# Adding the result onto the residual in DRAM with accumulating DMAs, and four reorderings, in a one-core encoder layer

## The chip, the cores and the metric

The kernel runs on one NeuronCore of a Trainium2 chip. The metric is device time in microseconds (us) of one execution. Three runs of the kernel before took 1187.17, 1188.81 and 1190.94 us; the median is 1188.81 us.

Engines are named as in the profile: PE is the matrix engine (PEld its weight loads), DVE, ACT and POOL are the vector, scalar and GpSimd engines, SP issues DMAs. SPq, ACTq and POOLq are the DMA queues of SP, ACT and POOL.

## What is computed

One layer of a streaming encoder on 1024 prompt frames and 64 frames of a running stream, 1088 columns together, all in float32. Cut to what matters here:

```
hn = rmsnorm(x, g_pre1)
z = hn @ w_in                                  # [gate | xa | u | v], 4 x 512 columns
xa_c = causal_dwconv(xa); h = rg_lru(xa_c)     # gates r, i: sigmoid of block-diagonal products of xa_c
ya = rmsnorm(h * gelu(gate), g_out_a)
yb = rmsnorm(u * (w_s @ layernorm(v) + b_s), g_out_b)
x  = x + rmsnorm([ya, yb] @ w_o, g_post1)      # residual
hn2 = rmsnorm(x, g_pre2)
f  = (gelu(conv(hn2 @ w_up)[:, :3072]) * conv(hn2 @ w_up)[:, 3072:]) @ w_down
x  = x + rmsnorm(f, g_post2)                   # the output y; w_down is 3072 x 1024
```

## The kernel before, in words

Features lie on the 128 partitions, frames along the free dimension (1088 columns). Every float32 operand of a product is split into two parts of a reduced float32 type, `hi` (a rounding copy on ACT, L140) and `lo` (the remainder, a subtraction on DVE, L142 or L144), and a product is three matmuls: hi by hi, hi by lo, lo by hi. So every weight tile (128 x 1024, 512 KB, name `wraw`) is loaded by a DMA on SP, then split into `whi` and `wlo` before PE can use it.

A scheduler places instructions: the kernel text says what depends on what, and each engine then gets a fixed list that it works through in order. A DMA in SP's list that waits holds up all DMAs behind it in that list, the weight loads too. All large tiles come from one pool of 47 buffers.

The stages, in order of time:

- **Front** (to about 45 us of the span). For each of 8 input tiles `xr` (544 KB) ACT and DVE make `xh` and `xl`, and PE forms v in two passes over k = 0 to 7 (`v_mm`); weights `w_v` come as three tiles of 512 KB, one for two k. `gate_const` (L351) makes the constant `cst` of the v gate from one matmul `wsum` and four DVE operations.
- **Mixers.** `xa_tile` makes xa and its convolution `xc` on DVE (L487 to L489) and splits it into `ch` and `cl` there (L491 to L493); `lru_gates` multiplies those on PE and takes sigmoids `r` and `ig` on ACT; `u_tile` first multiplies its gate by the row scale `rbt`, on POOL (L536). Then the output projection; `post1` forms the residual x and stores it to a DRAM buffer `xd` (L708).
- **Up-projection** (about 400 to 900 us), a Strassen-like scheme of 7 products; its gated results and their sums go to the DRAM buffer `bd`.
- **Down-projection** (about 880 us to the end), the same scheme: 7 products in the order of `DOWN` (L40), each named by its operand of `bd` and its weight part: A11, S2 = A21 + A22 - A11, S3, A22, A12, S1 = A21 + A22, S4 = A12 - S2. Each product has 6 steps n; a step is `down_step` (48 matmuls of 272 columns), then `wmake(n + 3)` (split of the weights), `bmake(n + 6)`, `wload(n + 4)` and `bload(n + 7)`. In the product S2 `wload` loads three tiles, `wmake` forms S1 and S2 on DVE and stores both to the DRAM buffer `sd` by POOL; the products S1 and S4 read them back. `down_evac` adds the products into the 8 accumulators `facc`.
- **Finish.** `finish` does a quarter of the columns: `load_xn` reads the residual back from `xd` (SP), one matmul group sums the squares, POOL takes the power -1/2, then for 8 row tiles DVE multiplies (L1120), POOL or DVE adds to the residual (L1121), and SP stores groups of three tiles to the output (L1097). Two quarters run during the sixth product, the third in the middle of the seventh, whose columns are done in two parts of 284 and 260 (`COLS2`; its PSUM tile is `lps`, that of the others `dps`). `finish_last` does the last quarter at the very end, on DVE and POOL together.

Of the kernel before, what the change touches and what calls it, by code (L numbers as in the profile page):

```python
# [14 lines left out]
P = 128  # L15
# [24 lines left out]
DOWN = [("B11", "A11"), ("T2", "S2"), ("T3", "S3"), ("T4", "A22"), ("B21", "A12"), ("T1", "S1"), ("B22", "S4")]  # L40
# [27 lines left out]
def layer_kernel(ctx: ExitStack, tc, xT, w_fm, w_v, w_o, w_up, w_down, w_g, w_s, par, bc, yT, small, vn_out):  # L68
# [332 lines left out]
    for k in range(1, KD):  # L401
# [3 lines left out]
        if k == 3:  # L405
            gate_const()
# [67 lines left out]
    def xa_tile(t, fill=()):  # L474
# [92 lines left out]
    def seq(*fs):  # L567
# [8 lines left out]
    lru_tile(1)  # L576
    u_tile(1)
    xa_tile(3, lru_gates(2))
    lru_tile(2)
    u_tile(2)  # L580
# [96 lines left out]
    xd = drp.tile([P, KD, T], F32, tag="xd", name="xd")  # L677
# [15 lines left out]
    def post1(c, mix, tiles, ssq):  # L693
# [8 lines left out]
        for m in range(KD):  # L702
# [276 lines left out]
    def wload(n):  # L979
# [6 lines left out]
        for src in {"A11": (a11,), "S2": (a21, a22, a11), "S3": (a11, a21), "A22": (a22,), "A12": (a12,),  # L986
# [5 lines left out]
    def wmake(n):  # L992
# [4 lines left out]
        src = raw[0]  # L997
        if DOWN[p][1] == "S2":
            a21, a22, a11 = raw
            nc.vector.tensor_tensor(a22, a21, a22, op=ALU.add)  # L1000
            nc.gpsimd.dma_start(sd[0, i], a22)
            nc.vector.tensor_tensor(a11, a22, a11, op=ALU.subtract)
            nc.gpsimd.dma_start(sd[1, i], a11)
            src = a11
        elif len(raw) == 2:
            nc.vector.tensor_tensor(raw[0], raw[0], raw[1], op=ALU.subtract)  # L1006
# [11 lines left out]
    for j in range(NPRE, NF):  # L1018
        hooks = ()
        if j == NF - 1:  # L1020
# [4 lines left out]
                     [call(bmake, 3), call(bload, 5), call(wmake, 2)])  # L1025
# [6 lines left out]
    wload(3)  # L1032
    bmake(5)
    bload(6)
# [27 lines left out]
    def down_evac(p, m, ps):  # L1062
# [6 lines left out]
        if p == 0:  # L1069
            facc[m] = big_tile(name="facc")[:, :T]  # L1070
            for c, (a, b) in enumerate(CC):
                with tc.high_priority(offset=PRI):
                    nc.scalar.activation(facc_cols(m, a, b), ps[c], AF.Copy)
        elif p == 1:
            add(m, 1, m, 0)
        elif p == 2:
            facc[m + 4] = big_tile(name="facc")[:, :T]
            add(m + 4, 1, m, 1)
        elif p == 3:
            add(m + 4, 0, m + 4, 1)  # L1080
        elif p == 4:
            add(m, 0, m, 0)
# [3 lines left out]
        if p == 3 or p == 5:  # L1086
            h = 0 if p == 3 else HT
            for a, b in CC:
                sq_add(m + 4, h + a, h + b)
        if p == 4:  # L1090
            for a, b in CC:
                sq_add(m, a, b)

    def out_dma(m, cols, xn, queue):
        if m % 3 == 2 or m == KD - 1:
            g, n = m // 3, m % 3 + 1
            queue.dma_start(yT[:, 3 * g:3 * g + n, cols], xn[g][:, :n, :])  # L1097

    def load_xn(cols):
        w = cols.stop - cols.start  # L1100
        xn = [big_tile(shape=(P, 3, w), name="xn") for _ in range(3)]
        for q in range(3):
            e = min(3 * q + 3, KD)
            nc.sync.dma_start(xn[q][:, :e - 3 * q, :], xd[:, 3 * q:e, cols])
        return xn

    def finish(cols, xn=None):
        w = cols.stop - cols.start
        xn = xn or load_xn(cols)
        yield  # L1110
# [6 lines left out]
        for m in range(KD):  # L1117
            f = facc[m][:, cols]
            x = xn[m // 3][:, m % 3, :]
            nc.vector.scalar_tensor_tensor(f, f, pv("g_post2", m), rr, op0=ALU.mult, op1=ALU.mult)  # L1120
            (nc.vector if m % 3 == 2 else nc.gpsimd).tensor_tensor(x, x, f, op=ALU.add)  # L1121
            out_dma(m, cols, xn, nc.sync)
            if m % 2 == 1:
                yield

    def scale_f(m, cols):
        f = facc[m][:, cols]
        nc.scalar.activation(f, f, AF.Copy, scale=pv("g_post2", m))

    def finish_last(cols, xn, more):  # L1130
# [5 lines left out]
        for n, m in enumerate(range(KD)):  # L1136
            f = facc[m][:, cols]
            x = xn[m // 3][:, m % 3, :]
            mul, add = LAST_ENG[m]
            e = {"v": nc.vector, "g": nc.gpsimd}  # L1140
# [21 lines left out]
    last_p = len(DOWN) - 1  # L1162
    for n in range(6 * last_p):
        if n == 6 * last_p - 6:
            gens2.append(finish(slice(*COLS1[0])))
# [120 lines left out]
```

## Time and profile before

| what | value |
|---|---|
| median of three runs | 1188.81 us |
| the profiled execution's own time | 1188.03 us |
| its span | 1186.3 us |
| PE busy, mean granted clock | 1137.9 us (96%), 0.983 |
| DVE, ACT, POOL busy | 861.6, 531.3, 178.2 us |
| HBM read, written | 110.65 MB, 38.85 MB |

PE is busy in 96% of the span, so a microsecond in which PE waits, or runs at the lower of its two clock levels, is nearly always a microsecond of the kernel. The other engines matter only where PE waits for them. The 48 us in which PE is not busy are at the two ends and in a few waits, which the rows below list.

### The profile page before, as it was taken

The page shows a single profiled execution, that of the slowest core. Times are in us where ns is not written, and L with a number is a line of the kernel's source. Part 1 is how long each engine was busy: PE and PEld are TensorE (multiplying, and loading weights), DVE is VectorE, ACT ScalarE, POOL GpSimd, SP SyncE. Part 2 cuts the span into 40 slices and gives each one's busy share as a digit, 9 for nine tenths or more (in the row PEclk, how much of TensorE's full clock was granted, in tenths as well). Part 3 has the DMA queues.
Part 4 walks back from the last instruction along what each step waited for, and adds up shares of the span by engine and source line. Part 5 has one row for each costly group of instructions (what it writes and reads, how often), then busy time and mean ns, then how long its engine had stood idle before and what let it go on. Part 6 is the DMA issues. An engine that isn't in the chain of part 4 may idle for free. (4 is left out here: it accounts for less than half of the span.)

```text
span 1186.3 us, 20679 instructions
## 1 busy us (share of the span) xinstructions
PE 1137.9 (96%) x8420; PEld 1115.8 (94%) x8420; DVE 861.6 (73%) x1374; ACT 531.3 (45%) x868; POOL 178.2 (15%) x292
## 2 busy tenths in 40 slices
PE   8998999999999999999999999999999999999675
PEld 6798999999998999999999999999999999999675
DVE  7567666866687889787887778778779574656745
ACT  7212567544445545444444445444464233433321
POOL 0214001110000122221021111111221100002203
PEclk9999999999999999999999999999999999999878
DMA  8110111221333132232132223223169985543562
GB/s 309 36 41 18 37 36 36 72 92 42 99 116 116 36 120 93 93 119 93 50 134 98 80 99 123 76 78 128 61 241 402 418 332 206 196 154 111 195 226 76
DMA packets 54000, 150.85 MB, mean 127 GB/s; under 512 B 5488, under 2 KB 22384, under 8 KB 53904
## 3 DMA queue, kind: packets, MB, share of 16 engines
q1 hardware_dynamic: 44784, 119.18, 28.8%
q0 software_dynamic: 8496, 29.81, 6.4%
q8 instruction: 66, 1.08, 0.4%
q10 hardware_dynamic: 624, 0.53, 0.2%
q14 instruction: 30, 0.25, 0.1%
HBM read 110.65 MB, written 38.85 MB: 126 GB/s over the span
## 5 line engine op out<-in xcount | busy, mean ns | idle before, releaser
L898 PE MATMUL up<-bh,wop 128*128 128x274 f32 x2464 | 472.7, 290 | 0.0
L898 PEld LDWEIGHTS up<-bh,wop 128*128 128x128 f32 x2464 | 389.4, 189 | 1.8 <-ACT uraw L912 1.3
L898 PE MATMUL up<-bl,wop 128*128 128x274 f32 x1232 | 356.8, 290 | 0.0
L898 PEld LDWEIGHTS up<-bl,wop 128*128 128x128 f32 x1232 | 233.3, 189 | 0.0
L1057 PE MATMUL dps<-gh,whi 128*128 128x272 f32 x576 | 121.1, 290 | 3.6 <-ACT whi L140 3.6
L1057 PE MATMUL dps<-gh,wlo 128*128 128x272 f32 x576 | 119.6, 290 | 0.9 <-DVE wlo L142 0.8
L1057 PE MATMUL dps<-gl,whi 128*128 128x272 f32 x576 | 120.4, 289 | 0.0
L140 ACT ACTIVATE whi<-wraw 128x1024 fp32r<-128x1024 f32 x70 | 73.0, 1050 | 87.3 <-DVE wraw L1006 37.2
L142 DVE TENSOR_TENSOR wlo<-wraw,whi 128x1024 fp32r<-128x1024 f32 x70 | 85.1, 1220 | 26.0 <-ACT whi L140 25.8
L140 ACT ACTIVATE wop<-wsum 128x512 fp32r<-128x512 f32 x88 | 53.0, 627 | 107.6 <-DVE wsum L854 105.3
L1057 PEld LDWEIGHTS dps<-gh,whi 128*128 128x128 f32 x576 | 91.2, 189 | 4.1 <-ACT whi L140 4.1
L912 ACT ACTIVATE uraw<-up 128x274 f32<-128x274 f32 x176 | 65.7, 389 | 64.6 <-PE up L898 64.2
L1057 PEld LDWEIGHTS dps<-gh,wlo 128*128 128x128 f32 x576 | 90.6, 189 | 1.8 <-DVE wlo L142 1.8
L1057 PEld LDWEIGHTS dps<-gl,whi 128*128 128x128 f32 x576 | 91.3, 190 | 0.0
L798 DVE SCALAR_TENSOR_TENSOR yg<-uraw,pt,yg 128x1090 f32<-128x1090 f32 (+1 forms) x48 | 64.8, 1350 | 26.5 <-ACT yg L796 26.5
L917 DVE TENSOR_TENSOR uraw<-up,uraw 128x274 f32<-128x274 f32 x132 | 56.3, 438 | 33.5 <-PE up L898 30.6
L641 PE MATMUL ops<-yh,whi 128*128 128x274 f32 (+1 forms) x256 | 75.2, 294 | 0.0
L641 PE MATMUL ops<-yl,whi 128*128 128x274 f32 (+1 forms) x256 | 73.8, 288 | 0.0
L641 PE MATMUL ops<-yh,wlo 128*128 128x274 f32 (+1 forms) x256 | 73.7, 288 | 0.0
L185 POOL TENSOR_TENSOR rs<-v,mhalf 92x3 f32<-92x3 f32 (+4 forms) x20 | 21.8, 1089 | 326.6 <-DVE v L184 326.6
L424 PE MATMUL ps<-xh,whi 128*128 128x364 f32 (+3 forms) x296 | 69.6, 330 | 0.0
L798 DVE SCALAR_TENSOR_TENSOR yv<-uraw,pt,yv 128x1090 f32<-128x1090 f32 (+1 forms) x48 | 64.7, 1347 | 4.8 <-ACT yv L796 4.6
(225 smaller groups left out, 2225.7 us busy)
## 6 DMA issues: line engine op xcount, KB each, us to landing
wraw<-in_w_down_dram SPq DMA_DIRECT2D x54, 512.0 KB, 8.3
wraw<-in_w_up_dram SPq DMA_DIRECT2D x48, 512.0 KB, 3.8
graw<-bd SPq DMA_DIRECT2D x42, 544.0 KB, 6.7
bd<-yg POOLq DMA_DIRECT2D x36, 272.0 KB, 3.1
bd<-ta POOLq DMA_DIRECT2D x24, 272.0 KB, 3.2
bd<-tb POOLq DMA_DIRECT2D x24, 272.0 KB, 3.2
wraw<-in_w_fm_dram SPq DMA_DIRECT2D x12, 512.0 KB, 3.5
sd<-wraw POOLq DMA_DIRECT2D x12, 512.0 KB, 7.6
```

The costliest lines, as they stand in the source:

```text
L140: nc.scalar.activation(hi, src, AF.Copy, scale=1.0 if scale is None else scale)
L142: nc.vector.tensor_tensor(lo, src, hi.bitcast(F32), op=ALU.subtract)
L185: nc.gpsimd.tensor_tensor(out, v[:n[0], :n[1]], mhalf[:n[0], :n[1]], op=ALU.pow)
L424: nc.tensor.matmul(ps[c], wt[:, k * P:(k + 1) * P], at[k][:, cols], start=(k == 0 and q == 0), stop=(k == KD - 1 and q == 2))
L641: nc.tensor.matmul(ps, wt[:, i * 256 + mi * P:i * 256 + (mi + 1) * P], a[k, c], start=(first and i == 0 and j == 0), stop=(last and i == 3 ...
L798: nc.vector.scalar_tensor_tensor(y[:, d:TG], x[:, :TG - d], tap(2 - d), y[:, d:TG], op0=ALU.mult, op1=ALU.add)
L898: nc.tensor.matmul(dst[c], wt[:, k * P:(k + 1) * P], at[:, fourth(k)], start=(start and k == 0 and q == 0), stop=(k == 3 and q == 2), skip ...
L912: nc.scalar.activation(dst[c], src[c], AF.Copy)
L917: nc.vector.tensor_tensor(dst[c], src[c], p[c], op=ALU.add)
L1057: nc.tensor.matmul(ps, wt[:, k * 256 + mi * P:k * 256 + (mi + 1) * P], at[:, o + a:o + b], start=(first and k == 0 and q == 0), stop=(last ...
```

## The change

`DOWN` is put in a new order, with the product A12 second and the product of S2 third. `operand(n)` makes weights one step sooner (`wmake(n + 4)`, `wload(n + 5)`). S1 is no longer formed on DVE: six DMAs on SP copy A21 from DRAM to `sd`, and six accumulating DMAs on POOL add A22 to it there. They are written in the loop of the up-projection, but the scheduler decides their place. The residual goes to the output tensor itself instead of `xd`; `finish` and `finish_last` scale their results and add them to it by accumulating DMAs on POOL, and the loads of `xn`, the adds and the stores on SP are gone. In the front `gate_const` comes at k = 1 instead of k = 3, the split of `xc` becomes a function of its own, `xa_split`, called later, the multiplication by `rbt` goes from POOL to DVE, and the first broadcast matmul of `rstd_tail` keeps its place in program order.

```diff
-DOWN = [("B11", "A11"), ("T2", "S2"), ("T3", "S3"), ("T4", "A22"), ("B21", "A12"), ("T1", "S1"), ("B22", "S4")]
+DOWN = [("B11", "A11"), ("B21", "A12"), ("T2", "S2"), ("T3", "S3"), ("T4", "A22"), ("T1", "S1"), ("B22", "S4")]
@@ rstd_tail
+            if b == 0:
+                tc.keep_in_program_order(mm)
@@ second pass of v
         if k == 1:
             stats_x()
-        if k == 3:
             gate_const()
@@ xa_tile
+        lru[t] = [xc]
+
+    def xa_split(t):
+        xc = lru[t][0]
         ch, cl = big_tile(F32R, name="ch"), big_tile(F32R, name="cl")
         for g, d in PIECES:
-            split(ch[:, d], cl[:, d], xc[:, g])
+            tc.keep_in_program_order(nc.scalar.activation(ch[:, d], xc[:, g], AF.Copy))
+            nc.vector.tensor_tensor(cl[:, d], xc[:, g], ch[:, d].bitcast(F32), op=ALU.subtract)
@@ u_tile
-        nc.gpsimd.tensor_tensor(sh, sh, rbt, op=ALU.mult)
+        nc.vector.tensor_tensor(sh, sh, rbt, op=ALU.mult)
@@ the calls
+    xa_split(0)
     xa_tile(1, ...)
-    u_tile(0, lru_gates(0))
+    u_tile(0, lru_gates(0) + [lambda: xa_split(1)])
...
@@ post1
-                nc.sync.dma_start(xd[:, 4 * g:4 * g + 4, qs(c)], v4(xt[g], w))
+                nc.sync.dma_start(yT[:, 4 * g:4 * g + 4, qs(c)], v4(xt[g], w))
@@ wload, wmake
-        for src in {"A11": (a11,), "S2": (a21, a22, a11), ...
+        for src in {"A11": (a11,), "S2": (s1, a11), ...
+        if len(raw) == 2:
+            nc.vector.tensor_tensor(src, src, raw[1], op=ALU.subtract)
         if DOWN[p][1] == "S2":
-            a21, a22, a11 = raw
-            nc.vector.tensor_tensor(a22, a21, a22, op=ALU.add)
-            nc.gpsimd.dma_start(sd[0, i], a22)
-            nc.vector.tensor_tensor(a11, a22, a11, op=ALU.subtract)
-            nc.gpsimd.dma_start(sd[1, i], a11)
-            src = a11
+            nc.gpsimd.dma_start(sd[1, i], src)
@@ loop of the up-projection, j = NPRE to NF - 1
+        i = j - NPRE - 2
+        if 0 <= i < 6:
+            nc.sync.dma_start(sd[0, i], w_down[1, 0, i])
+        if 1 <= i < 7:
+            nc.gpsimd.dma_start(sd[0, i - 1], w_down[1, 1, i - 1], accum_op=ALU.add, max_dma_last_dim=1024)
@@ finish
-        xn = xn or load_xn(cols)
-        yield
...
             nc.vector.scalar_tensor_tensor(f, f, pv("g_post2", m), rr, op0=ALU.mult, op1=ALU.mult)
-            (nc.vector if m % 3 == 2 else nc.gpsimd).tensor_tensor(x, x, f, op=ALU.add)
-            out_dma(m, cols, xn, nc.sync)
+            nc.gpsimd.dma_start(yT[:, m, cols], f, accum_op=ALU.add)
@@ finish_last
-            e[mul].tensor_tensor(f, f, bp if mul == "v" else rr, op=ALU.mult)
-            e[add].tensor_tensor(x, x, f, op=ALU.add)
-            out_dma(m, cols, xn, nc.scalar if m // 3 == 1 else nc.sync)
+        for g, q in ((1, nc.sync), (0, nc.scalar)):
+            for m in range(4):
+                f = fg[g][:, m, :]
+                nc.vector.tensor_tensor(f, f, bp, op=ALU.mult)
+            nc.gpsimd.dma_start(yT[:, 4 * g:4 * g + 4, cols], fg[g], accum_op=ALU.add)
@@ steps of the down-projection
+    def operand(n):
+        wmake(n + 4)
+        bmake(n + 6)
+        wload(n + 5)
+        bload(n + 7)
```

Left out of the diff: `down_evac` and `sq_add` follow the new order of the products (the first product is now copied to both halves of `facc` by 8 more ACT copies of 272 columns), and `scale_f` writes the last quarter into two packed tiles `fg`.

**SP, the first DMAs of the program.** `xr` are input tiles, `wraw` weights, `sd` is the DRAM buffer of S1 and S2. Before, from the sixth DMA on:

```order
L302 DMA pt<-in_par_dram 128x432
L321 DMA xr<-in_xT_dram 128x1088 x2
L166 DMA wraw<-in_w_v_dram 128x1024 x3
L166 DMA wraw<-in_w_g_dram 128x1024
L321 DMA xr<-in_xT_dram 128x1088 x2
```

Now, from the same DMA on:

```order
L304 DMA pt<-in_par_dram 128x432
L1031 DMA sd<-in_w_down_dram 16x8192 x2
L323 DMA xr<-in_xT_dram 128x1088
L1031 DMA sd<-in_w_down_dram 16x8192 x2
L323 DMA xr<-in_xT_dram 128x1088
L1031 DMA sd<-in_w_down_dram 16x8192 x2
L166 DMA wraw<-in_w_v_dram 128x1024 x3
L166 DMA wraw<-in_w_g_dram 128x1024
L323 DMA xr<-in_xT_dram 128x1088 x2
```

The six copies of A21 (512 KB each) stand at the head of the program: two ahead of the input tile of k = 1, four ahead of that of k = 2, six ahead of the weights of k = 2. The six accumulating DMAs are now the first DMAs of POOL's list, each behind the copy that it adds to.

**SP, the loads around the last product.** `graw` is the operand from `bd`, `xn` the residual, `out_dram` the output. Before:

```order
L1104 DMA xn<-xd 128x3x272 x2
L1104 DMA xn<-xd 128x2x272
L1097 DMA out_dram<-xn 128x3x272
L989 DMA wraw<-in_w_down_dram 128x1024
L989 DMA wraw<-sd 128x1024
L972 DMA graw<-bd 128x1088
L1097 DMA out_dram<-xn 128x3x272
L1097 DMA out_dram<-xn 128x2x272
L989 DMA wraw<-in_w_down_dram 128x1024
L989 DMA wraw<-sd 128x1024
```

Now:

```order
L997 DMA wraw<-in_w_down_dram 128x1024
L997 DMA wraw<-sd 128x1024
L980 DMA graw<-bd 128x1088
L997 DMA wraw<-in_w_down_dram 128x1024
L997 DMA wraw<-sd 128x1024
L980 DMA graw<-bd 128x1088
```

In the down-projection SP's list now holds loads of operands alone; the additions to the output are DMAs of POOL.

**ACT, the gates of the first head group.** `ch` is the rounded `xc` of the tile in question, `r` and `ig` the sigmoids that free the PSUM tile `gps`. Before:

```order
L140 ACTIVATE ch<-xc 128x1024
L140 ACTIVATE ch<-xc 128x64
L140 ACTIVATE whi<-wraw 128x1024
L140 ACTIVATE ch<-xc 128x1024
L140 ACTIVATE ch<-xc 128x64
L140 ACTIVATE whi<-wraw 128x1024
L507 ACT_TABLE_LOAD
L507 ACTIVATE r<-gps,pt 128x364 x2
```

Now:

```order
L498 ACTIVATE ch<-xc 128x1024
L498 ACTIVATE ch<-xc 128x64
L140 ACTIVATE whi<-wraw 128x1024 x2
L513 ACT_TABLE_LOAD
L513 ACTIVATE r<-gps,pt 128x364 x2
```

The split of the second tile's `xc` no longer stands ahead of the first tile's sigmoids; it comes behind all six of them.

## Rows read from the trace of the kernel before

**Rows 1.** Page, the span in 40 slices of 29.7 us, in tenths.

```profile
DMA  8110111221333132232132223223169985543562
```

**Rows 2.** Waits of PE, largest: waiter, released by, total us, times, longest us.

```profile
PE lps L1057 <- ACT whi L140: 16.0, 4, 7.1
PE gps L505 <- ACT r L507: 3.7, 1, 3.7
PE dps L1057 <- ACT whi L140: 3.6, 3, 1.8
PE bp L392 <- DVE cst L355: 2.9, 1, 2.9
```

**Rows 3.** Windows of PE: stretch, us, busy (instructions), granted clock, DMA share, GB/s.

```profile
1088.60:1092.60 4.00, 3.96 (x19) 0.57 0.99 334
...
1121.40:1126.40 5.00, 4.97 (x19) 0.50 0.86 257
1130.30:1136.70 6.40, 6.19 (x23) 0.50 1.07 382
1140.80:1146.80 6.00, 5.98 (x25) 0.50 0.69 238
1150.00:1155.00 5.00, 5.00 (x42) 1.00 0.01 3
```

**Rows 4.** Waits of SP's DMA queue from 880 us on.

```profile
SPq L1097 <- DVE xn L1121: 68.9, 5, 30.4
```

**Rows 5.** Timeline of SP, 1057 to 1088 us: start, us, instruction.

```profile
1058.29 1.56 SPq L1104 DMA_DIRECT2D xn<-xd  x3
1086.13 0.96 SPq L1097 DMA_DIRECT2D out_dram<-xn  x2
1087.18 0.53 SPq L989 DMA_DIRECT2D wraw<-sd  x1
```

**Rows 6.** Timeline of DVE, 1112 to 1122 us.

```profile
1113.19 5.39 DVE L1120 SCALAR_TENSOR_TENSOR facc<-facc,pt,rrf 128x272 f32<-128x272 f32 x8
```

**Rows 7.** Windows of all: us, PE, PEld, DVE, ACT, POOL busy, PE clock, DMA, GB/s.

```profile
8.00:17.00 9.00, 8.31 (x32) 6.32 (x31) 7.70 (x22) 8.29 (x12) 0.00 (x0) 1.00 1.02 415
17.00:26.00 9.00, 8.93 (x39) 6.95 (x38) 9.00 (x9) 6.46 (x7) 0.31 (x1) 1.00 1.03 354
...
900.00:960.00 60.00, 58.11 (x455) 57.03 (x454) 41.57 (x41) 17.79 (x22) 7.70 (x15) 1.00 1.02 411
```

**Rows 8.** Timeline of ACT, front: the splits of `w_v` and of a late input tile.

```profile
13.37 3.05 ACT L140 ACTIVATE whi<-wraw 128x1024 fp32r<-128x1024 f32 x3
...
25.22 1.21 ACT L140 ACTIVATE xh<-xr,gp 128x1088 fp32r<-128x1088 f32 x1 [1.97 <-DMA xr<-in_xT_dram]
```

**Rows 9.** Timeline of PE, front: the first matmuls of k = 2 and k = 5.

```profile
16.91 0.40 PE L288 MATMUL vps<-whi,xh 128*128 128x512 f32 x1
...
29.78 0.86 PE L288 MATMUL vps<-whi,xh 128*128 128x512 f32 x3
```

**Rows 10.** Timeline, 96 to 115 us: POOL, DVE and PE around the first gates.

```profile
96.30 11.65 POOL L536 TENSOR_TENSOR s<-s,rbt 128x1088 f32<-128x1088 f32 x4 [9.87 <-DVE s L383]
...
102.05 8.44 DVE L489 SCALAR_TENSOR_TENSOR xc<-xa,pt,xc 128x1090 f32<-128x1090 f32 x3
...
114.61 0.43 PE L505 MATMUL gps<-ch,whi 128*128 128x360 f32 x1 [3.73 <-ACT r L507]
```

**Rows 11.** Window just behind that wait, columns as in rows 7.

```profile
115.50:119.90 4.40, 4.40 (x18) 4.12 (x17) 1.21 (x1) 2.10 (x4) 0.00 (x0) 0.61 0.00 0
```

**Rows 12.** Page, another operation of that form: count, busy us, mean ns.

```profile
L798 DVE SCALAR_TENSOR_TENSOR yg<-uraw,pt,yg 128x1090 f32<-128x1090 f32 (+1 forms) x48 | 64.8, 1350 | 26.5 <-ACT yg L796 26.5
```

**Rows 13.** Timeline of DVE, end: first and last operations behind the sum of squares.

```profile
1177.68 0.76 DVE L1141 TENSOR_TENSOR facc<-facc,bp 128x260 f32<-128x260 f32 x2 [2.41 <-ACT rrf L207]
...
1182.27 0.73 DVE L1142 TENSOR_TENSOR xn<-xn,facc 128x260 f32<-128x260 f32 x1
```

**Rows 14.** DMA issues, 1173 to 1187 us: KB each, median us to landing.

```profile
out_dram<-xn SPq DMA_DIRECT2D x1, 390.0 KB, 2.7
```

More of the change, by code (lines that the diff above doesn't have):

```diff
@@ L576, in layer_kernel @@
     lru_tile(1)
+    xa_split(2)
     u_tile(1)
@@ L579, in layer_kernel @@
     lru_tile(2)
+    xa_split(3)
     u_tile(2)
@@ L675, in o_mm @@
         return mix, tiles, ssq
-    xd = drp.tile([P, KD, T], F32, tag="xd", name="xd")
     hn = {}
@@ L985, in wload @@
         wraw[n] = []
-        for src in {"A11": (a11,), "S2": (a21, a22, a11), "S3": (a11, a21), "A22": (a22,), "A12": (a12,),
+        for src in {"A11": (a11,), "S2": (s1, a11), "S3": (a11, a21), "A22": (a22,), "A12": (a12,),
                     "S1": (s1,), "S4": (a12, s2)}[DOWN[p][1]]:
@@ L1031, in layer_kernel @@
     opb.clear()
-    wload(3)
+    wmake(2)
     bmake(5)
+    wload(4)
+    wmake(3)
     bload(6)
@@ L1070, in down_evac @@
             facc[m] = big_tile(name="facc")[:, :T]
-            for c, (a, b) in enumerate(CC):
-                with tc.high_priority(offset=PRI):
-                    nc.scalar.activation(facc_cols(m, a, b), ps[c], AF.Copy)
+            for h in range(2):
+                for c, (a, b) in enumerate(CC):
+                    with tc.high_priority(offset=PRI):
+                        nc.scalar.activation(facc_cols(m, h * HT + a, h * HT + b), ps[c], AF.Copy)
         elif p == 1:
-            add(m, 1, m, 0)
+            add(m, 0, m, 0)
         elif p == 2:
+            add(m, 1, m, 1)
+        elif p == 3:
             facc[m + 4] = big_tile(name="facc")[:, :T]
             add(m + 4, 1, m, 1)
-        elif p == 3:
+        elif p == 4:
             add(m + 4, 0, m + 4, 1)
-        elif p == 4:
-            add(m, 0, m, 0)
         elif p == 5:
@@ L1085, in down_evac, with finish @@
             add(m, 1, m, 1)
-        if p == 3 or p == 5:
-            h = 0 if p == 3 else HT
+        if p in (1, 4, 5):
+            d, h = {1: (m, 0), 4: (m + 4, 0), 5: (m + 4, HT)}[p]
             for a, b in CC:
[L1089 to L1099, printed above, removed]
-        w = cols.stop - cols.start
[L1101 to L1108, printed above, removed]
-        xn = xn or load_xn(cols)
-        yield
+                sq_add(d, h + a, h + b)
+    def finish(cols):
+        w = cols.stop - cols.start
         head = rstd_head(ssqt[0][:, cols], D)
@@ L1118, in finish, with finish_last @@
             f = facc[m][:, cols]
[L1119 removed]
             nc.vector.scalar_tensor_tensor(f, f, pv("g_post2", m), rr, op0=ALU.mult, op1=ALU.mult)
[L1121 to L1122 removed]
+            nc.gpsimd.dma_start(yT[:, m, cols], f, accum_op=ALU.add)
             if m % 2 == 1:
                 yield
+    fg = {}
     def scale_f(m, cols):
[L1127 to L1130 removed]
+        nc.scalar.activation(fg[m // 4][:, m % 4, :], facc[m][:, cols], AF.Copy, scale=pv("g_post2", m))
+    def finish_last(cols, more):
         w = cols.stop - cols.start
@@ L1162, in layer_kernel @@
     last_p = len(DOWN) - 1
+    def operand(n):
[3 more added lines that the diff above has]
+        bload(n + 7)
     for n in range(6 * last_p):
         if n == 6 * last_p - 6:
-            gens2.append(finish(slice(*COLS1[0])))
-            gens2.append(finish(slice(*COLS1[1])))
+            for c in COLS1:
+                gens2.append(finish(slice(*c)))
         down_step(n)
-        wmake(n + 3)
-        bmake(n + 6)
-        wload(n + 4)
-        bload(n + 7)
+        operand(n)
         if n == 0:
@@ L1179, in layer_kernel @@
         w = hi - lo
-        xn = load_xn(cols)
         if r == 1:
+            for g in range(2):
+                fg[g] = big_tile(name="fg")[:, :4 * w].rearrange("p (m t) -> p m t", m=4)
             for m in range(4, KD):
@@ L1188, in layer_kernel @@
                 if r == 0 and m % 2 == 0:
-                    wmake(n + 3)
-                    wload(n + 4)
+                    operand(n)
                 for k in range(4):
@@ L1204, in layer_kernel @@
         if r == 0:
-            gens2.append(finish(cols, xn))
+            gens2.append(finish(cols))
     while gens2:
         tick2()
-    finish_last(cols, xn, more)
+    finish_last(cols, more)
 def _lay(inp, np):
```

15 lines of the change are left out of this document (4 added, 11 removed).

## The prediction

> **What bounds the kernel now.** I read the page's slices first, then the waits of PE, then the timelines around its longest waits, then the queue of SP. PE is busy in 96% of the span, so what counts is where it waits and where its clock is low. The slices show DMA busy throughout in two places: the first 30 us, and the down-projection [rows 1].
>
> The waits of PE name the weights: in the last product it waits 16.0 us, in four pieces of up to 7.1, for `whi`; in the other products of the down-projection 3.6 us [rows 2]. Behind each wait at the end there is a stretch at a granted clock of 0.50 to 0.57, the 1.2 GHz level, after PE had stood still: 4.0, 5.0, 6.4 and 6.0 us [rows 3]. At 0.50 it does 19 matmuls in 5 us, at 1.00 42 (a little shorter ones), so such a stretch gives about half: lost are 4.0 x 0.43 + (5.0 + 6.4 + 6.0) x 0.5 = 10.4 us.
>
> Why are the weights late? SP's queue waits 68.9 us in five stores of `xn` for the adds on POOL and DVE [rows 4]. Its timeline shows what that holds up: after the `xn` loads at 1058.29 nothing is issued until 1086.13, when the stores go, and the weight load behind them goes at 1087.18 [rows 5]. A smaller part is DVE: eight multiplies of `finish` stand as one block of 5.39 us ahead of a subtraction for S4 that PE waits for [rows 6].
>
> **The change part by part.**
>
> *Loads freed of the stores (the residual added by DMA, operands a step sooner).* SP's list in the down-projection now holds operand loads alone, so the 28 us of blocked queue go. `operand` makes weights four steps ahead, not three; a step is 48 matmuls at 0.12 us (42 in 5 us [rows 3]), some 6 us more of lead, longer than the block of 5.39 us. DVE also loses its adds to `xn` and, in the product S2, one subtraction per step. What goes at most: 16.0 + 3.6 + 10.4 = 30.0 us. What is late next can only be DVE in the sixth product, which still holds 16 such multiplies; I leave one wait with its cold stretch, 3 us. **-27**, bounds -30 and -14 (only the blocked queue goes, DVE still stops PE: half).
>
> *S1 by DMA.* In the down-projection this takes traffic out of a stretch in which DMA is full, 411 GB/s [rows 7]; its waits are counted above. The price is in the front, because the order puts six copies of 0.52 MB, 3.1 MB, and behind them six accumulating DMAs of the same size, at the head of the queues. There DMA is full already: 1.02 and 1.0x in 8 to 26 us at 415 and 354 GB/s [rows 7]. A copy costs at that rate 0.52 / 0.415 = 1.26 us, six 7.6 us. The trace has no DMA from DRAM to DRAM and none that accumulates. Bounds for the six accumulations: nothing (they only fill gaps) to twice a copy, 15.1 us, since they read two streams; below zero is excluded, as they only add traffic. I take once, 7.6 us, nearest to the rows.
>
> Who waits: all six copies are ahead of the weights of k = 2. ACT starts their split at 13.37 [rows 8], and PE begins k = 2 at 16.91 [rows 9]; 7.6 us later the split begins at 21.0 and `whi` is there at 22.0 (3.05 / 3), so PE loses 5.1 us without any accumulation. With them the later tiles decide: the tile of k = 5 arrives at 25.22 (ACT waits for it [rows 8]), and PE wants it at 29.78 [rows 9]; less 1.2 us for the split, it may come 3.4 us later for nothing. So the loss is 7.6 + 7.6 - 3.4 = 11.8 us, at most 7.6 + 15.1 - 3.4 = 19.3. Nothing takes it up again, since PE is nearly never idle in the stages behind. **+12**, bounds +5 and +19.
>
> The Trainium skill, *DMA: Bandwidth & Descriptors*, section "Queues, rings and completion order", says that each DMA engine takes turns between the queues that have work for it, packet by packet. With halves for SP and POOL the input tiles would come at half rate from the first accumulation on; that is rival C. The trace does not show such a case.
>
> *Order of the front.* Two waits of PE are touched. At the v gate PE waits 2.9 us for `cst` [rows 2]; `gate_const` now comes two k sooner, so the broadcast finds its PSUM tile free. At 114.61 PE waits 3.7 us for ACT's `r` [rows 10]. The row above tells why: three DVE steps of the convolution take 8.44 us, 2.81 each, while POOL runs its four multiplies by `rbt` for 11.65 us [rows 10]; the same form takes 1.35 elsewhere [rows 12]. ACT's list has the split of that `xc` ahead of the sigmoids. Both causes go: the split stands behind the sigmoids, the multiplies are on DVE. They cost DVE about 4 x 1.3 us there, hidden while PE works on the next tile. Behind that wait the clock is 0.61 for 4.4 us [rows 11], 1.7 us more. Sum 2.9 + 3.7 + 1.7 = 8.3; I keep 1 for new waits by moved DVE work. **-7**, bounds -8.3 and 0.
>
> *The end.* Before, DVE works from 1177.68 to 1183.0 on eight multiplies and adds [rows 13], shared with POOL, and the last store ends the span 3.3 us later. Now eight multiplies at 0.38 us (0.76 for two): the first four end at 1179.2, the last at 1180.7, on the old clock. Two accumulating DMAs of 532 KB follow. A plain store of 390 KB lands in 2.7 us [rows 14], so 532 KB at that pace in 3.7, and the end would be 1184.4, 1.9 sooner. At half that pace the two in a row need 2 x 3.7 x 2 = 14.8 from 1179.2 on, 1194: 7.7 later. I take **+1**, nearer the plain store. The quarters before it add by 24 DMAs beside PE work; nobody waits for them. The ACT copies of the first product (8 more) lie beside its 36 us of matmuls: 0.
>
> Sum against the profiled execution's own 1188.0: 1188.0 - 27 + 12 - 7 + 1 = 1167.0. The median of the runs is 0.8 above the profiled execution, so **1168**.
>
> **Rivals.**
>
> A (the forecast): 1168.
>
> B: the accumulations take almost nothing from the input tiles, so only the six copies count, +5 instead of +12: 1161. For it: each waits for its copy, and DMA has room after 26 us. Against: the copies are done well before.
>
> C: the queues share in halves until the accumulations are done, +19: 1175. For it: both are then full.
>
> D: DVE becomes what the last two products wait for. The 16 multiplies take 2 x 5.4 = 11 us of the sixth product's 36, and a block of them stood in front of a wait of 7.1 us before [rows 6, 2]. Half of the 27 stays: 1168 + 13 = 1181. Against it: the longer lead.
>
> E, slower than before: accumulating DMAs are slow, in one place above all, the end. The third quarter (8 x 145 KB) and the last two DMAs, 2.2 MB, must land behind about 1165 on the old clock, 21 us before the old end. At a rate r they need 2.2 MB / r; the front then pays +19 as in C. Without the end the sum is 1188 - 27 - 7 + 19 = 1173, so slower needs over 15 us at the end: 2.2 MB in 21 + 15 = 36 us, r under 60 GB/s, a sixth of a plain DMA's rate here. At 50 GB/s: 44 us, +23, about 1197. Nothing in the trace speaks for so low a rate, nothing excludes it.
>
> **How the numbers follow.** Chances: A 0.50, B 0.17, C 0.15, D 0.11, E 0.07. A's own range, 1162 to 1173. The range to hold 8 in 10 leaves out E, the upper half of D, and B's low end with the end of the program 2 us sooner: 1157 to 1181. A measurement of this kernel tells a difference from about 0.3%, 3.6 us: faster is below 1185.2, slower above 1192.4. A, B, C and nearly all of D are faster: 0.91; E is mostly slower: 0.06; same 0.03.
>
> **What would show it.** Right: SP in the down-projection without stores and without gaps of 28 us; PE's waits for `whi` under `lps` gone or under 3 us; a clock of 1.00 through the last product; DMA full to about 40 us instead of 26, and PE waiting for `xr` or `w_v` splits in the front for some 12 us, k = 2 first; no wait of 3.7 us at the gates. Wrong: if PE's front waits grow by less than 5 or more than 19 us (B, or a cost that I don't see), if DVE is busy without a gap through the sixth product with PE waiting (D), or if the last DMAs take over 10 us behind DVE's last multiply (E).

## The result, and the profile after

The changed kernel took 1175.75 us (median of four runs, 1174.22 to 1177.59); the kernel before, run beside it, 1189.88 us (four runs). The ratio is 0.9889, with a 95% interval of 0.9865 to 0.9913: 13.2 us faster, of the 21 that were forecast. The profiled execution took 1176.07 us, its span 1173.9.

The start times of the first and last matmuls of each stage (of a product, those of `hi` by `hi`) divide the 12.4 us of the span; the stretch up to the first `up` holds the mixers, the output projection and the up-projection's first matmuls (`pps`):

| stretch of PE's time | before, us | after, us | difference | forecast |
|---|---|---|---|---|
| start to the last `vps<-w0h,x0h` (second pass of v) | 43.8 | 58.3 | +14.5 | +12 |
| from there to the first `up` | 364.2 | 356.9 | -7.3 | -7 |
| up-projection, the rest (first `up` to first `dps`) | 473.2 | 472.7 | -0.5 | 0 |
| six products (first to last `dps`) | 225.5 | 220.2 | -5.3 | } |
| seventh product (last `dps` to last `lps`) | 65.7 | 48.0 | -17.7 | } -27 |
| last `lps` to the end of the span | 13.9 | 17.8 | +3.9 | +1 |

The waits of PE in the changed kernel (waiter, released by, total us, times, longest) answer to [rows 2]:

```profile
PE vps L290 <- ACT whi L140: 5.4, 1, 5.4
PE vps L290 <- ACT xh L140: 5.4, 3, 2.3
PE vps L284 <- ACT w0h L140: 4.8, 1, 4.8
PE lps L1067 <- ACT gh L140: 4.0, 1, 4.0
...
PE dps L1067 <- ACT whi L140: 0.5, 1, 0.5
```

The 16.0 us of `lps` for `whi`, the 3.7 for `r` and the 2.9 for `cst` are gone, and 0.5 of the 3.6 of `dps` is left. In their place stand four waits in the front, 10.8 us together, for `whi` and `xh`, and one of 4.0 us in the last product; the 4.8 for `w0h` is the start of the program, 5.1 before.

**Front.** The slices of the page (29.35 us each) show DMA at 8 tenths in the second slice, where [rows 1] had 1:

```profile
DMA  9811111140224123221322332232256779555925
```

The timeline of ACT shows the weights of k = 2 and the input tile of k = 5, which [rows 8] had at 13.37 and 25.22:

```profile
21.73 1.06 ACT L140 ACTIVATE whi<-wraw 128x1024 fp32r<-128x1024 f32 x1 [4.19 <-DMA wraw<-in_w_v_dram]
...
40.86 1.20 ACT L140 ACTIVATE xh<-xr,gp 128x1088 fp32r<-128x1088 f32 x1 [5.05 <-DMA xr<-in_xT_dram]
```

They come 8.4 and 15.6 us later. PE's timeline in the same stretch, to be held against [rows 9]; in brackets is the idle time before the instruction and what ended it:

```profile
13.00 1.66 PE L290 MATMUL vps<-w0h,xh 128*128 128x512 f32 x6 [1.34 <-ACT xh L140]
22.84 0.79 PE L290 MATMUL vps<-whi,xh 128*128 128x512 f32 x1 [5.38 <-ACT whi L140]
31.74 1.66 PE L290 MATMUL vps<-whi,xh 128*128 128x512 f32 x6 [2.25 <-ACT xh L140]
42.11 0.96 PE L290 MATMUL vps<-whi,xh 128*128 128x512 f32 x3 [1.76 <-ACT xh L140]
43.50 0.50 PE L290 MATMUL vps<-whi,xl 128*128 128x512 f32 x1 [0.43 <-DVE xl L144]
```

The five waits are 11.2 us, 10.1 more than before (which had 0.7 for `xl` here, and a first wait longer by 0.3). The windows give the rest (columns as in [rows 7]):

```profile
22.80:27.00 4.20, 4.12 (x9) 2.82 (x10) 2.45 (x2) 1.83 (x2) 1.04 (x1) 0.50 1.12 327
...
42.10:48.00 5.90, 5.46 (x16) 4.07 (x17) 5.90 (x5) 4.77 (x5) 0.00 (x0) 0.71 1.15 277
48.00:54.00 6.00, 6.00 (x28) 4.91 (x27) 1.60 (x2) 0.56 (x1) 0.00 (x0) 1.00 0.65 103
```

Behind the wait of 5.4 us the granted clock is 0.50, the 1.2 GHz level, and behind the last waits 0.71. At 1.00 PE does 28 matmuls in 6 us; so the 9 and the 16 lost 4.12 - 9 x 0.214 = 2.2 us and 5.46 - 16 x 0.214 = 2.0 us. Waits and cold clock make 14.3 of the 14.5 us.

**Down-projection.** SP waits for buffers that PE frees, and no longer for `xn` ([rows 4] had 68.9 us there):

```profile
SPq L997 <- PE dps L1067: 115.1, 25, 14.6
```

DVE, in the stretch of [rows 6]: the block of multiplies is there still, six in place of eight, and the subtraction for S4 (L1007) right behind it.

```profile
1114.80 2.56 DVE L1112 SCALAR_TENSOR_TENSOR facc<-facc,pt,rrf 128x272 f32<-128x272 f32 x6
1117.28 1.22 DVE L1007 TENSOR_TENSOR wraw<-wraw 128x1024 f32<-128x1024 f32 x1
```

Windows around PE's wait of 4.0 us, which ends at 1120.6:

```profile
1120.60:1126.60 6.00, 5.34 (x21) 4.89 (x21) 4.88 (x5) 2.06 (x2) 0.32 (x1) 0.52 0.49 64
1126.60:1132.60 6.00, 5.93 (x46) 5.81 (x46) 3.46 (x7) 1.95 (x3) 0.00 (x0) 1.00 0.00 0
```

One cold stretch of some 6 us is left of the four of [rows 3]; in the second window PE does 46 matmuls where it did 21 in the first.

**End.** DVE's last eight multiplies, and POOL's two issues, where [rows 13] had multiplies and adds:

```profile
1161.45 2.77 DVE L1131 TENSOR_TENSOR fg<-fg,bp 128x260 f32<-128x260 f32 x8 [2.60 <-ACT rrf L209]
```

```profile
1163.18 2.70 POOL L1132 DMA_DIRECT2D out_dram<-fg  x2 [3.37 <-DVE fg L1131]
```

The DMA issues from 1150 us on (KB each, median us to landing), where [rows 14] had 2.7 us for 390 KB:

```profile
out_dram<-facc POOLq DMA_DIRECT2D x8, 142.0 KB, 5.1
out_dram<-fg POOLq DMA_DIRECT2D x2, 520.0 KB, 6.9
```

DVE is done at 1164.2, and the span ends 9.7 us later; before it ended 3.3 us behind DVE.

### The profile page after: what moved, and what is told of

Its sections match the earlier page's. It is cut to its first block, busy times and chain, and to the rows that moved or that the text cites. A ratio compares the mean times of both kernels' runs of the same rounds, so it can differ in the third digit from the quotient of the medians.

```text
span 1173.9 us, 20616 instructions
## 1 busy us (share of the span) xinstructions
PE 1132.0 (96%) x8420; PEld 1109.0 (94%) x8420; DVE 841.0 (72%) x1363; ACT 534.2 (46%) x876; POOL 172.0 (15%) x291
## 4 chain that ended last, share of the span: by engine, by line
PE 86%; issue 6%; DMA 3%; DVE 2%; POOL 1%; ACT 1%; SPq 0%; POOLq 0%; DVEq 0%; ACTq 0%
PE up L906 40%; PE dps L1067 16%; PE ps L425 12%; PE ops L650 7%; PE pps L775 4%; PE vps L290 2%; DMA xr<-in_xT_dram 1%; DMA wraw<-in_w_v_dram 1%; PE gps L511 1%; PE bp L205 1%; POOL out_dram L1113 1%; PE sp L382 1%; PE st L193 1%; DVE gl L142 1%; ACT whi L140 1%
## 5 line engine op out<-in xcount | busy, mean ns | idle before, releaser
L142 DVE TENSOR_TENSOR wlo<-wraw,whi 128x1024 fp32r<-128x1024 f32 x70 | 85.4, 1221 | 35.4 <-ACT whi L140 34.8
L425 PE MATMUL ps<-xh,wlo 128*128 128x364 f32 (+3 forms) x296 | 67.6, 324 | 0.0
```

The lines of the kernel that those rows point to most:

```text
L142: nc.vector.tensor_tensor(lo, src, hi.bitcast(F32), op=ALU.subtract)
L425: nc.tensor.matmul(ps[c], wt[:, k * P:(k + 1) * P], at[k][:, cols], start=(k == 0 and q == 0), stop=(k == KD - 1 and q == 2))
```

## The experiments

The theory: the S1 DMAs at the head of the queues cost the 14.5 us of the front, of which copies and accumulations are about half each; the front orders are worth 7; the down-projection's 23 us come from SP's queue and the longer lead; the accumulating DMAs at the end cost 4. The rivals are named with each. Times are medians, ratios are to the kernel before in the same group. Three groups ran on three chips (e1 to e4, e5 to e8, e9 to e12): kernels are compared directly inside a group, else by the ratio, with 1190 us for the kernel before. The intervals of two ratios together leave such a difference open by 3 to 4 us. A stretch of a profile comes from one execution, and is good to about 2 us: e1_late and e12_late_again are the same kernel, and take 50.0 and 48.0 us in the seventh product.

**The copies and accumulations where the code has them** (e1_late).

```diff
-            nc.sync.dma_start(sd[0, i], w_down[1, 0, i])
+            tc.keep_in_program_order(nc.sync.dma_start(sd[0, i], w_down[1, 0, i]))
...
+            tc.keep_in_program_order(nc.gpsimd.dma_start(sd[0, i - 1], ..., accum_op=ALU.add, ...))
```

> The changed kernel, but the six copies and six accumulating DMAs that form S1 keep the place at which they are written, in the loop of the up-projection. Theory: they cost the front 14.5 us (PE begins its second v pass at 58 us of the span instead of 44), and there is room for them later: 1175.8 - 14.5 = 1161 us, second pass at 44. Rival 1: the front is late because of its moved orders (gate_const, split of xc), so nothing changes: 1176. Rival 2: POOL, waiting for a copy, holds up the stores of the up-projection and PE waits there: 1165 to 1175, with waits of PE under up.

1164.21 us, ratio 0.978 (0.9754 to 0.9806): (0.9889 - 0.978) x 1190 = 13 us less than the changed kernel. The last `vps<-w0h,x0h` starts at 44.5 us (43.8 before the change, 58.3 in the changed kernel). Both rivals fall: the moved orders, which this kernel keeps, do not make the front late, and the transfers cost PE nothing in the up-projection (472.6 us, against 472.7). Their price in the front was their place alone.

**The copies alone** (e2_copies). It leaves out the accumulations, so that S1 is A21 alone.

```diff
-        if 1 <= i < 7:
-            nc.gpsimd.dma_start(sd[0, i - 1], w_down[1, 1, i - 1], accum_op=ALU.add, max_dma_last_dim=1024)
```

> The changed kernel without the six accumulating DMAs (S1 is then A21 alone; the copies stay at the head of SP's queue). Theory: the copies cost the front 5 us and the accumulations the other 9 to 10, so the second v pass begins at about 49 us of the span and the time is 1166. Rival: the copies, being ahead in the queue, are the whole cost, accumulations fill gaps: 58 us and 1176.

1168.9 us, ratio 0.9823 (0.9804 to 0.9841), 7.9 us less than the changed kernel. The second pass starts at 51.4: the copies cost 51.4 - 43.8 = 7.6 us, the accumulations 58.3 - 51.4 = 6.9. In the other kernels with both at the head of the queues this start lies between 56.4 and 59.5, in those with neither between 43.1 and 44.9, so that "about half each" holds, and more than that is not shown. PE's waits in its front, in the columns used above:

```profile
PE vps L290 <- ACT whi L140: 2.5, 1, 2.5
PE vps L290 <- ACT xh L140: 2.3, 1, 2.3
```

**The front orders of before** (e3_front; besides the lines shown, the split of `xc` is back in `xa_tile` and the broadcast has no fixed place).

```diff
         if k == 1:
             stats_x()
-            gate_const()
+        if k == 3:
+            gate_const()
...
-        nc.vector.tensor_tensor(sh, sh, rbt, op=ALU.mult)
+        nc.gpsimd.tensor_tensor(sh, sh, rbt, op=ALU.mult)
```

> The changed kernel with the front orders of before (gate_const at k = 3, split of xc inside xa_tile, multiplication by rbt on POOL, no fixed place of the broadcast matmul). Theory: PE waits again 2.9 us for cst and 3.7 us for r with 1.7 us at the low clock behind: 7.5 us more, 1183. Rival: shifted by the late front, these waits would have gone anyway, since DVE and POOL run ahead: 1176.

1187.48 us, ratio 0.9974 (0.9959 to 0.9989): 0.0085 x 1190 = 10 us more than the changed kernel, not 7. In the profile the stretch from the second pass to the first `up` is 367.7 us, 10.8 more. The surplus is not in the mixers. A window of 77 us near the end of that stretch, with the end of the output projection and most of `pps`, has a granted clock of 1.00 in the changed kernel; here it reads (columns as in [rows 7])

```profile
339.50:416.50 77.00, 74.09 (x578) 73.44 (x577) 57.81 (x113) 35.17 (x69) 5.90 (x8) 0.96 0.32 101
```

A clock of 0.96 in place of 1.00 is 0.04 x 77 = 3 us. This is not of the old orders' making: e12_late_again, which has the new ones, shows it too, with less loss.

```profile
324.90:401.90 77.00, 74.02 (x581) 73.37 (x580) 64.97 (x121) 37.33 (x70) 9.04 (x13) 0.98 0.28 92
```

The same edit on top of e1_late (e10_front_late) was run to see whether the DMAs in the front had a part in it.

> The kernel of e1_late (S1's DMAs in the up-projection) with the front orders of before put back. It prices the front orders without S1's traffic in the front. If they are worth the 7 us predicted (2.9 + 3.7 + 1.7 - 1): e1 + 7, 1171, with PE's waits of 2.9 us for cst and 3.7 us for r back. If they are worth the 11 to 12 us that e3_front showed, whatever the traffic: 1175 to 1176. In the second case the prediction's term was undersized; in the first the 4 to 5 us more of e3_front came from S1's DMAs beside the old order.

1169.64 us (0.9856, 0.9833 to 0.9879) against 1162.31 for e12_late_again beside it: +7.3. So the orders are worth about the 7 forecast, and what e3_front showed beyond it did not repeat. In all profiles the stretch from the second pass to the first `up` is 356.9 to 361.0 us with the new orders and 364.3 to 367.7 with the old. The old wait is back in e10_front_late, and a smaller one for `cst`:

```profile
PE gps L505 <- ACT r L507: 3.7, 1, 3.7
PE bp L392 <- DVE cst L355: 1.3, 1, 1.3
```

**The lead of before** (e4_lead3).

```diff
-    wload(4)
-    wmake(3)
...
-        wmake(n + 4)
+        wmake(n + 3)
         bmake(n + 6)
-        wload(n + 5)
+        wload(n + 4)
```

The first two lines stand ahead of the products and start the lead.

> The changed kernel with weights made three steps ahead again (wmake(n + 3), wload(n + 4)). Theory: the 23 us won in the down-projection come from SP's queue, freed of the stores; the longer lead only covers DVE's blocks: at most 4 us more, 1176 to 1180. Rival: the longer lead brings half or more: 1187 or above, with PE waits for whi under lps as before.

1185.13 us, ratio 0.9955 (0.9936 to 0.9974), 7.9 more. The last product takes 54.4 us from the last `dps` on (48.0), and PE's longest waits there are

```profile
PE lps L1065 <- ACT whi L140: 9.4, 3, 5.2
```

The upper end of the expectation was passed, and the rival's half of the 23 us not reached: in the profile 6.4 of the 17.7 us won in the last product are lost again when the lead alone is taken back.

**The result handled as before** (e5_out_before: `xd`, loads of `xn`, adds on POOL and DVE, stores by SP; the lead of four stays).

```diff
+        xn = xn or load_xn(cols)
...
-            nc.gpsimd.dma_start(yT[:, m, cols], f, accum_op=ALU.add)
+            (nc.vector if m % 3 == 2 else nc.gpsimd).tensor_tensor(x, x, f, op=ALU.add)
+            out_dma(m, cols, xn, nc.sync)
```

> The changed kernel with the handling of the result as before: the residual goes to the scratch xd, comes back by SP loads of xn, is added on POOL and DVE, and SP (for the end SP and ACT) stores the sums. Everything else stays changed: operands four steps ahead, S1 by DMA, the order of products, the front. Theory (the freed SP queue is most of what the down-projection gained, the lead about 7 to 9 us of 23): some 14 to 16 us of the down-projection come back, PE waits for whi of lps rise from 4 to over 10 us, and the end is 4 us sooner: 1185 to 1189. Rival (a lead of four steps hides the blocked queue as well, so the accumulating DMAs gain nothing beyond it): only the end moves, 1171 to 1176.

1185.03 us, ratio 0.9961 (0.9945 to 0.9977), against 0.9889 for the changed kernel: 8.6 us more. The last product takes 57.7 us, 9.7 more, and the end 14.9, 2.9 less. PE's waits there:

```profile
PE lps L1068 <- ACT whi L140: 6.1, 2, 3.6
PE lps L1068 <- ACT gh L140: 2.6, 1, 2.6
```

The waits of SP's queue from 880 us on have the stores back, as in [rows 4]:

```profile
SPq L1106 <- DVE xn L1130: 67.9, 6, 24.9
```

and DVE, while POOL adds to `xn` from 1114.94 to 1120.85, is slower:

```profile
1113.36 1.22 DVE L1008 TENSOR_TENSOR wraw<-wraw 128x1024 f32<-128x1024 f32 x1
...
1115.75 1.78 DVE L142 TENSOR_TENSOR wlo<-wraw,whi 128x1024 fp32r<-128x1024 f32 x1
1117.46 1.85 DVE L142 TENSOR_TENSOR gl<-graw,gh 128x1088 fp32r<-128x1088 f32 x1
```

`wlo` and `gl` take 1.22 and 1.28 elsewhere. This is a second thing that the accumulating DMAs removed, and the prediction did not have it; what it costs PE apart from SP's queue was not tried. So result handling and lead are both needed in the last product: 9.7 and 6.4 us, each taken back alone, of the 17.7 that go when both are taken back, in the kernel before.

Neither run moves the first six products (219.5 and 221.1 us, against 220.2). Of their 5.3 us, 3.8 lie in the sixth product (42.2 us before, 38.4 after). Before, PE waits there twice, just behind the stretch in which SP's queue stands still until 1086.13 [rows 5], and the clock behind is 0.57 [rows 3]:

```profile
1086.61 0.52 PE L1057 MATMUL dps<-gh,whi 128*128 128x272 f32 x2 [1.82 <-ACT whi L140]
1088.64 0.55 PE L1057 MATMUL dps<-gh,wlo 128*128 128x272 f32 x2 [0.76 <-DVE wlo L142]
```

These waits stay away in e5_out_before, where the queue is blocked again but the lead is four steps, and in e4_lead3, where the lead is three but the queue is free. The likeliest reading is that here either of the two is enough; that something which both runs keep does it (the order of the products, the step of S2 with one load and one subtraction less) is not ruled out. What takes the other 1.5 us out of the first five products was not tried.

**The last quarter stored plainly** (e6_end_plain, and on top of e1_late e11_late_plain): the residual is read back from the output tensor while PE works, added on DVE and POOL, stored by SP and ACT.

```diff
+            xn = load_xn(cols)
...
-            nc.gpsimd.dma_start(yT[:, 4 * g:4 * g + 4, cols], fg[g], accum_op=ALU.add)
+            e[add].tensor_tensor(x, x, f, op=ALU.add)
+            out_dma(m, cols, xn, nc.scalar if m // 3 == 1 else nc.sync)
```

> The changed kernel, but the last quarter of the columns does not accumulate in DRAM: its residual is read back from yT into xn while PE works on it, added on DVE and POOL, and stored by plain DMAs on SP and ACT, as before. Theory (two accumulating DMAs of 520 KB behind DVE's last multiply are what made the end 17.6 us instead of 13.7 from the last matmul on): -3 to -5, about 1172. Rival (the extra reads and adds in the last product cost as much as the end gains, or the span ends with the third quarter's accumulations anyway): 1175 to 1178.

> e1_late and the plain store of the last quarter, without the shift of the second quarter's multiplies. Against e12_late_again on the same chip: if two accumulating DMAs at the end cost 3.9 us (the profiles of after and e6_end_plain), 3 to 5 us less than it; if the end's gain is given back elsewhere (e6_end_plain's times did not move), within 1.5 us of it.

> e1_late once more, as the kernel that the three others of this group are compared with on one chip: 1162 to 1166.

e6_end_plain 1175.83 us, ratio 0.9887 (0.9868 to 0.9905), no difference to the changed kernel. e11_late_plain 1161.29, 0.9768 (0.9751 to 0.9785), against e12_late_again 1162.31, 0.9782 (0.9765 to 0.98). In the profiles the end is 13.9 us in e6_end_plain (17.8 in the changed kernel) and 13.8 in e11_late_plain (17.3 in e12_late_again), so 3.5 to 3.9 shorter; the last product is longer, 48.9 against 48.0 and 49.2 against 48.0. The sum of these two is -2.3 to -3.0, and the times show 0.2 and 1.0 us, within their intervals. The accumulating DMAs cost the end some 3.5 us; the gain of taking them away is smaller, and not distinguished from nothing.

**The multiplies of the second quarter moved behind the subtractions for S4** (e7_defer).

```diff
-            for c in COLS1:
-                gens2.append(finish(slice(*c)))
+            gens2.append(finish(slice(*COLS1[0])))
...
+            if r == 0 and m == 2:
+                gens2.append(finish(slice(*COLS1[1])))
```

> The changed kernel, but the eight multiplies of finish for the second quarter start later, at m = 2 of the last product, behind all subtractions for S4. Theory (the block of six multiplies, 2.56 us, ahead of the subtraction of S4 is the cause of PE's wait of 4.0 us for gh): that wait is gone or under 1 us, with part of the colder stretch behind it, -4 to -7: 1169 to 1172. Rival 1 (the loads of S4 are late, and the multiplies only stood in the gap): the wait stays at 3 us or more, 1175 to 1177. Rival 2 (the accumulations of two quarters now pile up at the end): the wait goes but the end grows by as much, 1174 to 1178.

1177.17 us, ratio 0.9904 (0.9883 to 0.9924): no gain, and the theory falls. The block is gone from DVE's list, and the wait of 4.0 us for `gh` is 1.8 in two pieces; yet all waits of `lps` are 5.1 us in seven pieces, against 5.5 in four without the edit. DVE's timeline shows what stands in their place:

```profile
1108.80 1.22 DVE L1007 TENSOR_TENSOR wraw<-wraw 128x1024 f32<-128x1024 f32 x1
...
1113.55 1.22 DVE L1007 TENSOR_TENSOR wraw<-wraw 128x1024 f32<-128x1024 f32 x1
1115.95 1.23 DVE L142 TENSOR_TENSOR wlo<-wraw,whi 128x1024 fp32r<-128x1024 f32 x1 [1.18 <-ACT whi L140]
1117.09 1.28 DVE L142 TENSOR_TENSOR gl<-graw,gh 128x1088 fp32r<-128x1088 f32 x1
1118.29 1.22 DVE L1007 TENSOR_TENSOR wraw<-wraw 128x1024 f32<-128x1024 f32 x1
```

Subtractions follow each other at 4.75 us. In that time DVE subtracts, waits 1.18 for ACT's `whi`, and splits twice; the next subtraction stands behind. A step of the first row tile takes PE 12 matmuls, 1.6 us. So the chain of one operand, not the block, is what PE meets at the start of this last product. This is read from the timeline: no run shortens the chain by itself, since the one that was to do so (e9_pool, below) met another cost.

**All three edits** (e8_all: e1_late, e6_end_plain, e7_defer).

> The changed kernel with three edits at once: copies and accumulations of S1 issued in the up-projection as written, the last quarter stored plainly, the second quarter's multiplies behind the subtractions for S4. If the three costs are apart from each other: 1164 (late S1 alone) - 4 - 5 = 1155. If only the late S1 counts: 1162 to 1165. If the late accumulations or the plain end collide with the rest: above 1165.

1158.27 us (1156.48 to 1160.51), ratio 0.9737 (0.9718 to 0.9756), the fastest of all kernels here: 29.5 us below the 1187.81 of the kernel before beside it, and (0.9889 - 0.9737) x 1188 = 18 us faster than the change. Against e11_late_plain's 0.9768 the intervals overlap, so that the moved multiplies have a part in it is not shown.

**The last four subtractions for S4 on POOL** (e9_pool, on top of e8_all).

```diff
-            nc.vector.tensor_tensor(src, src, raw[1], op=ALU.subtract)
+            (nc.gpsimd if n >= 38 else nc.vector).tensor_tensor(src, src, raw[1], op=ALU.subtract)
```

> The three edits of e8_all, and the last four subtractions for S4 on POOL instead of DVE. Theory (what PE still waits for in the last product, some 4 us in pieces, is a chain of 4.75 us per operand: DVE's subtraction, ACT's whi and gh, DVE's wlo and gl, one operand behind the other): with the subtraction on POOL the chain falls to about 3.7 us of DVE and ACT per operand, the waits of lps to 1 to 2 us, 2 to 4 us less than e11_late_plain and e8_all in the last product. Rival (the loads of S4 come late, since SP waits for buffers that PE frees, or POOL's subtraction takes 3 us or more): the waits stay near 4 us, within 1 us of e11_late_plain.

1164.66 us, ratio 0.9797 (0.978 to 0.9813): slower than e11_late_plain beside it by 3.4 us, by the ratios 7 us slower than e8_all, on which it is built, and neither theory said so. The timelines of POOL and DVE:

```profile
1099.64 9.25 POOL L1007 TENSOR_TENSOR wraw<-wraw 128x1024 f32<-128x1024 f32 x4
```

```profile
1099.20 10.78 DVE L142 TENSOR_TENSOR wlo<-wraw,whi 128x1024 fp32r<-128x1024 f32 x1
1109.90 1.28 DVE L142 TENSOR_TENSOR gl<-graw,gh 128x1088 fp32r<-128x1088 f32 x1
```

One DVE split that takes 1.22 us elsewhere took 10.78, and ended 1.1 us behind POOL's four subtractions. PE waited 10.0 us for it:

```profile
PE lps L1068 <- DVE wlo L142: 10.0, 1, 10.0
```

A smaller part is at the end: POOL's power for the last quarter stands behind 13 accumulating DMAs of POOL, and PE waits 2.8 us for it, where the longest such wait of the changed kernel is 1.3.

## Why the prediction was right, and where its sizes were off

Faster by over 0.3% was forecast with 0.91, and it is so; 1175.75 lies in the range and above A's own (1162 to 1173), close to C's number but not by C's mechanism. Every part went in the direction given; three of the four terms were too hopeful, by 2.5 + 4.0 + 2.9 us, two rows came out better by 0.3 + 0.5, and that makes 8.6 of the 9.1 us between the sum (1167.0) and the profiled execution (1176.07).

*S1 by DMA, +12: +14.5.* The mechanism was right, and the arrivals nearly held to the number: the tile of k = 5 was to come at 25.22 + 15.2 = 40.4 and came at 40.86; `whi` of k = 2 was to be there at 22.0, and PE went on at 22.84. The term left out the clock behind the waits, which the down-projection's term had counted: 4.2 us. "Once a copy" for the accumulations was right as a loss to PE (6.9 us, copies 7.6), and B, which had them at almost nothing, is out; but that it came out at once a copy is in part luck. For its bytes an accumulation took the DMA engines 2.4 times as long as a plain DMA (below), over the bound of twice, and only 1.8 of the 3.1 MB had been moved when the tile of k = 5 came.

*Rival C.* Its number, 1175, was met, its halves were not. From 18 to 44 us both queues had work all the time:

```profile
q1 hardware_dynamic: 1834, 6.23, 65.9%
q0 software_dynamic: 1837, 1.83, 44.1%
```

The columns are packets, MB and share of the DMA engines' time; q1 is SP's queue, q0 that of the accumulations. SP's queue moved 6.23 MB in 26 us, 240 GB/s, where it had 415 and 354 in [rows 7]: 0.58 and 0.68 of it, not a half. The Trainium skill's rule (*DMA: Bandwidth & Descriptors*, "Queues, rings and completion order"), turns packet by packet, agrees with the packet counts, 1834 and 1837. That it makes halves of the bandwidth was the prediction's own step, and the packets differ: about 1.0 KB in q0, 3.4 in q1.

*Front orders, -7: -7.3,* and +7.3 when they alone are undone (e10_front_late), 10 in e3_front. The waits for `r` and `cst` are gone.

*Loads freed and a longer lead, -27: -23.0.* The cause was right, and the runs price its parts: in the last product 9.7 us the result's handling (SP's queue, and POOL's adds beside DVE, not told apart) and 6.4 the lead; the 5.3 of the first six products no run took back. "One wait with its cold stretch, 3 us" was undersized: PE waits 5.5 us in the last product and loses 5.34 - 21 x 0.129 = 2.6 more at 0.52 (46 matmuls in 5.93 us at 1.00). The prediction's reason for D, the block of multiplies, was wrong: without it the sum of the waits stays. What is late next is, by the timeline, the chain of subtraction and splits of each operand, 4.75 us; whether loads for which SP waits until PE frees a buffer add to it was not tried. The sum of DVE's work in the sixth product, from which D was argued, does not show such a chain. So the sign of a clock of 1.00 through the last product was not met.

*The end, +1: +3.9.* The plain pace that was taken, 3.7 us for 532 KB, was the wrong row to be near to: 520 KB took 6.9 us, close to the upper bound's half pace (7.4). The two overlap, so that the end came 3.8 us sooner than the upper bound of +7.7. The sign named for E, over 10 us behind DVE's last multiply, was nearly met, at 9.7, without E: that needed a rate under 60 GB/s, and some 160 to 200 was measured (below).

## What to carry to other kernels

A DMA without a dependency goes where the scheduler has room in the list, not where the code has it: price it at the head of the queue, or fix its place; here that was worth 13 us, as much as the whole change. Allow for a cold stretch behind each wait of PE that a new transfer makes, in every stage. Where operands for the next product are made in a chain across two engines, compare the time per operand in that chain with the time in which PE uses one; the engine's busy sum hides it. Where two parts of a change guard against the same wait, taking back one alone can show nothing.

## What the runs showed of the hardware

- An accumulating DMA from DRAM to DRAM (packets of 1 KB) takes 35.4 / 2.15 = 16.5% per MB of the DMA engines' time from 8 to 46 us, plain ones 71.7 / 10.32 = 6.9%: 2.4 times as much.

```profile
q1 hardware_dynamic: 2396, 10.32, 71.7%
q0 software_dynamic: 2162, 2.15, 35.4%
```

- An issue of an accumulating DMA that stands alone holds POOL 0.86 to 1.35 us; six in a row hold it 5.32. At the end, with nothing beside them, the accumulations of the result keep the DMA engines full at some 160 to 200 GB/s, where plain loads reach 411 [rows 7].
- Four `tensor_tensor` of POOL held up one of DVE for their whole length (10.78 in place of 1.22 us, in e9_pool). The Trainium skill (*Advanced Engine Details and Errata*, "GPSIMD Details") says that POOL and DVE share a read and a write interface, with conflicts where DVE has two inputs in SBUF; this DVE operation has two, and the trace agrees. The same shows in e5_out_before above, and in [rows 6], where eight multiplies beside POOL take 0.67 us each and six now 0.43. It also explains [rows 10] better than the mean of 2.81 us did: single steps there take 3.51, 3.51 and, once POOL is done, 1.35.
- The granted clock is not the same for the same waits. Where the up-projection begins (`pps`), PE waits three times, 0.7 to 1.3 us, in every kernel here; behind them the clock stays at 1.00 in the profile of the changed kernel, and falls for a few us in those of e12_late_again and e3_front (the windows of 77 us above). In e7_defer, with waits of up to 1.6 us, it stays at 1.00 through the start of the last product; in e8_all, with none for an operand over 0.94, it is 0.72 to 0.89 for 18 us. What makes the difference is open.

Windows of e8_all and of e7_defer at the same place, columns as in [rows 7]:

```profile
1100.10:1106.10 6.00, 4.99 (x23) 4.52 (x24) 4.81 (x5) 2.06 (x2) 0.00 (x0) 0.72 0.17 57
1106.10:1112.10 6.00, 4.55 (x25) 3.85 (x26) 3.34 (x3) 2.06 (x2) 0.00 (x0) 0.89 0.00 0
1112.10:1118.10 6.00, 6.00 (x42) 6.00 (x41) 3.88 (x6) 1.94 (x3) 0.00 (x0) 0.82 0.00 0
```

```profile
1113.00:1119.00 6.00, 3.47 (x25) 3.01 (x24) 4.82 (x5) 2.06 (x2) 0.00 (x0) 1.00 0.01 3
1119.00:1125.00 6.00, 4.54 (x31) 3.84 (x30) 3.60 (x5) 2.38 (x3) 0.00 (x0) 1.00 0.00 0
1125.00:1131.00 6.00, 6.00 (x50) 6.00 (x49) 4.56 (x6) 1.65 (x4) 0.00 (x0) 1.00 0.00 0
```

In the third window of each PE does not wait at all, and does 42 matmuls in the one, 50 in the other.
